# Softmax values in two f32r passes, projections in quarters, sink attention ahead of the latent heads

## The chip, the cores and the metric

One core of one Trainium2 chip runs the whole kernel in one launch. The metric is the device time of one execution in microseconds; the median of three runs counts. Engines are named as in the profile: PE is TensorE, with PEld its weight loads, DVE VectorE, ACT ScalarE, POOL GpSimd, SP the queue that issues the DMAs.

## The reference, cut to what matters

Two decoder layers over 512 tokens of width 1024, all in float32. Each layer is a mixing block and a SwiGLU feed-forward of width 2816, with RMS norms before and after each. Layer 0 mixes with eight heads of windowed softmax attention (heads A, width 64) and four heads of gated linear attention (B). Layer 1 mixes with eight query heads over two key-value heads with a window of 128 and a sink logit (C, the sink attention), and with eight latent heads (D). For heads A and D the part that the change touches is, per head:

```python
# A: a table holds slope * distance and the logarithm of how many of three patterns see a key
# D: a table holds the causal mask
s = q @ k.T * scale - table
p = softmax(s)                 # 512 queries x 512 keys, causal
o = p @ v                      # v: 512 x 64
# D: queries and keys come from latents
q = rmsnorm(h @ w_q_latent) @ w_uq      # latent of 384 = 3 tiles of 128
k, v = rmsnorm(h @ w_kv_latent) @ w_ukv # latent of 256 = 2 tiles of 128
# and k gets a rotary part that all heads share
```

## The kernel before

Activations are held transposed: 1024 channels as 8 tiles of 128 partitions, 512 tokens in the free dimension. Nearly every product is made to float32 accuracy from two float32r parts: `split` casts a tensor to f32r on ACT (the high part) and subtracts that from the source on DVE (the low part), and `mm3` adds three products, high-high, high-low, low-high. `proj` makes 128 outputs for all tokens with 24 matmuls of 512 columns. Weights come by DMA on SP into `raw` (4 buffers), are split two items ahead of use (`weights`, `fill`), and lie in `wt` (8 buffers) in the order of the list `items`.

Heads A and D go through `Units`: each head has four units, one per block of 128 queries, over the 1 to 4 key blocks up to it. The first step (`head_first`) makes the scores (PE, for A in two f32r passes over stacked parts, for D in f32), adds the table and takes the row minimum (DVE), exponentiates with a row sum (ACT), takes the reciprocal and scales the row (DVE, line 401). The second step (`head_second`) transposes each block on PE (line 407, f32) and copies it out of PSUM (ACT, line 409). The third step multiplies with the values (line 413): f32, the stationary operand is V of one head, 64 columns, the moving one 128 queries, one matmul for each key block. An f32 matmul runs as two instructions. The two heads of a pair fill the two halves of one bank, which is then split for the output projection. The second step runs `LAG` = 4 units behind the first, the third `LAG2` = 2 behind the second.

In layer 0 the query and key projections of the next pair come in one block of 48 matmuls after the third unit of a pair (`A_NEXT`). In layer 1 the latents, the shared rotary key, the sink queries, keys and values, and the latent values come first, then heads D with one unit of the sink attention (8 units, four heads and a query block each) after every third unit, and the projections of the next pair after its fourth unit (`C_EVERY`, `D_NEXT`).

The order written is a priority. The framework schedules each engine's instructions with it: a later instruction whose inputs are ready and that has a buffer may go ahead of an earlier one that waits. The order is fixed when the program is built; at run time each engine works through its list in order and waits by semaphores. Buffers that matter: PSUM has 8 banks, two under the tag `ps` (projections, the first token block of an output projection) and six under `pa` (scores, transposes, values); SBUF has 28 cells of 128 x 512 (`CELLS`) for queries, keys, probabilities, latents and most of what is short-lived; 8 pages of 4 x 512; two gain buffers of 1024.

After the heads, `out_rows` multiplies the mixed heads with the output weights: three rows of weights over all token blocks, and the last five token block by token block, so that norms of one block run beside products of the next.

## Time and profile before

| | us |
|---|---|
| median of three runs | 1229.32 (1229.27 to 1230.81) |
| profiled execution, first to last instruction | 1227.8 |
| PE busy | 1213.7 |
| DVE busy | 551.7 |
| ACT busy | 472.2 |
| POOL busy | 56.5 |

The profiled execution's own time is its span, 1227.8 us; what lies around a span is in the runs' times and not in it. Busy time is the union of an engine's instructions; since matmuls overlap, PE's says only that it is never without one. The softmax of layer 0 lies at about 155 to 235 us, that of layer 1 at about 716 to 819 us; the feed-forwards fill most of the rest.

### The profile page before, as it was taken

The page shows a single profiled execution, that of the slowest core. Times are in us where ns is not written, and L with a number is a line of the kernel's source. Part 1 is how long each engine was busy: PE and PEld are TensorE (multiplying, and loading weights), DVE is VectorE, ACT ScalarE, POOL GpSimd, SP SyncE. Part 2 cuts the span into 40 slices and gives each one's busy share as a digit, 9 for nine tenths or more (in the row PEclk, how much of TensorE's full clock was granted, in tenths as well). Part 3 has the DMA queues.
Part 4 walks back from the last instruction along what each step waited for, and adds up shares of the span by engine and source line. Part 5 has one row for each costly group of instructions (what it writes and reads, how often), then busy time and mean ns, then how long its engine had stood idle before and what let it go on. Part 6 is the DMA issues. An engine that isn't in the chain of part 4 may idle for free.

```text
span 1227.8 us, 15007 instructions
## 1 busy us (share of the span) xinstructions
PE 1213.7 (99%) x5952; PEld 1000.5 (81%) x5952; DVE 551.7 (45%) x963; ACT 472.2 (38%) x858; POOL 56.5 (5%) x91
## 2 busy tenths in 40 slices
PE   8999999999999999999999999999999999999997
PEld 6787777789888888888889877778988888888886
DVE  5633566554333333323355577866433333332313
ACT  5424465633332322312235457764323233232211
POOL 2000111010000000000010011101000000000000
PEclk9999999999999999999999999999999999999999
DMA  7432121223233233233503230032232323323311
GB/s 272 124 100 72 35 70 52 82 74 103 88 102 99 90 103 94 95 103 106 186 1 104 97 107 22 19 108 81 87 89 100 104 89 100 103 86 103 114 41 69
DMA packets 32760, 112.76 MB, mean 92 GB/s; under 512 B 4753, under 2 KB 4913, under 8 KB 32690
## 3 DMA queue, kind: packets, MB, share of 16 engines
q1 hardware_dynamic: 32690, 111.80, 28.8%
q8 instruction: 47, 0.77, 0.3%
q14 instruction: 23, 0.19, 0.0%
HBM read 109.69 MB, written 2.10 MB: 91 GB/s over the span
## 4 chain that ended last, share of the span: by engine, by line
PE 96%; DVE 2%; ACT 1%; issue 0%; DMA 0%; POOL 0%; DVEq 0%; POOLq 0%; SPq 0%; ACTq 0%
PE pg L195 12%; PE pg L193 12%; PE pg L194 12%; PE y L194 9%; PE y L195 9%; PE y L193 9%; PE avt L413 4%; PE sc L378 3%; PE pf L194 2%; PE pf L195 2%; PE pf L193 2%; PE pt L407 1%; PE pq L193 1%; PE pq L194 1%; PE tp L257 1%; PE pq L195 1%
## 5 line engine op out<-in xcount | busy, mean ns | idle before, releaser
L109 ACT CAST whi<-raw 128x1024 fp32r<-128x1024 f32 (+2 forms) x211 | 198.4, 955 | 508.5 <-PE pg L194 300.1
L110 DVE TENSOR_TENSOR wlo<-raw,whi 128x1024 fp32r<-128x1024 f32 (+2 forms) x210 | 230.3, 1111 | 336.1 <-ACT whi L109 324.9
L193 PE MATMUL pg<-hf0h,whi 128*128 128x512 f32 x320 | 124.5, 389 | 0.0
L193 PE MATMUL pg<-hf1h,whi 128*128 128x512 f32 x320 | 124.5, 389 | 0.0
L194 PE MATMUL pg<-hf1l,whi 128*128 128x512 f32 x320 | 124.5, 389 | 0.0
L194 PE MATMUL pg<-hf0l,whi 128*128 128x512 f32 x320 | 124.5, 389 | 0.0
L195 PE MATMUL pg<-hf0h,wlo 128*128 128x512 f32 x320 | 124.5, 389 | 0.0
L195 PE MATMUL pg<-hf1h,wlo 128*128 128x512 f32 x320 | 124.5, 389 | 0.0
L328 DVE TENSOR_TENSOR sg<-sg,pg 128x512 f32<-128x512 f32 x40 | 27.5, 688 | 135.4 <-PE pg L195 135.4
L193 PE MATMUL y<-whi,gh 128*128 128x512 f32 x224 | 87.1, 389 | 0.0
L194 PE MATMUL y<-wlo,gh 128*128 128x512 f32 x224 | 87.1, 389 | 0.0
L195 PE MATMUL y<-whi,gl 128*128 128x512 f32 x224 | 87.1, 389 | 0.0
L195 PEld LDWEIGHTS pg<-hf0h,wlo 128*128 128x128 f32 x320 | 60.1, 188 | 12.6
L194 PEld LDWEIGHTS pg<-hf1l,whi 128*128 128x128 f32 x320 | 60.1, 188 | 12.5
L194 PEld LDWEIGHTS pg<-hf0l,whi 128*128 128x128 f32 x320 | 60.1, 188 | 12.5
L193 PEld LDWEIGHTS pg<-hf1h,whi 128*128 128x128 f32 x320 | 60.1, 188 | 12.4
L195 PEld LDWEIGHTS pg<-hf1h,wlo 128*128 128x128 f32 x320 | 60.1, 188 | 12.3
L193 PEld LDWEIGHTS pg<-hf0h,whi 128*128 128x128 f32 x320 | 60.1, 188 | 12.2
L230 POOL TENSOR_TENSOR rs<-ms,mhalf 128x1 f32<-128x1 f32 x32 | 17.7, 554 | 851.2 <-DVE ms L228 851.2
L270 ACT ACTIVATE junk<-y 128x512 f32<-128x512 f32 x32 | 19.1, 597 | 86.4 <-PE y L195 84.9
L193 PE MATMUL y<-whi,gph 128*128 128x512 f32 x128 | 50.0, 390 | 0.0
L195 PE MATMUL y<-whi,gpl 128*128 128x512 f32 x128 | 49.8, 389 | 0.0
(337 smaller groups left out, 2291.2 us busy)
## 6 DMA issues: line engine op xcount, KB each, us to landing
raw<-in_gu_dram SPq DMA_DIRECT2D x88, 512.0 KB, 3.5
raw<-in_ffn_w_down_dram SPq DMA_DIRECT2D x44, 512.0 KB, 3.5
raw<-in_w0s_dram SPq DMA_DIRECT2D x16, 512.0 KB, 3.5
raw<-in_w1s_dram SPq DMA_DIRECT2D x11, 512.0 KB, 3.5
raw<-in_w0m_dram SPq DMA_DIRECT2D x8, 512.0 KB, 3.8
raw<-in_ab_w_out_dram SPq DMA_DIRECT2D x8, 512.0 KB, 3.5
raw<-in_cd_w_out_dram SPq DMA_DIRECT2D x8, 512.0 KB, 3.5
x<-in_x_dram SPq DMA_DIRECT2D x4, 512.0 KB, 5.9
```

The source lines that it names most:

```text
L109: nc.scalar.copy(hi, src)
L110: return (eng or nc.vector).tensor_tensor(out=lo, in0=src, in1=hi.bitcast(F32), op=ALU.subtract)
L193: nc.tensor.matmul(ps, wh, xh, start=first, stop=False)
L194: nc.tensor.matmul(ps, wh, xl, start=False, stop=False)
L195: nc.tensor.matmul(ps, wl, xh, start=False, stop=last)
L230: nc.gpsimd.tensor_tensor(out=r, in0=t, in1=mhalf, op=ALU.pow)
L257: nc.tensor.transpose(ps[:, k, :], h[:, tok(4 * i + k)], ident)
L270: nc.scalar.activation(junk, ys[j], AF.Square, scale=1.0 / 32, accum_out=ss[:, i:i + 1])
L328: nc.vector.tensor_tensor(out=t, in0=t, in1=pu, op=ALU.mult)
L378: nc.tensor.matmul(sc, q, k, start=(i == 0), stop=(i == len(ks) - 1))
L407: nc.tensor.transpose(pt[:, j, :], p[:, tok(j)], ident)
L413: nc.tensor.matmul(out_ap, v(j), t[:, j, :], start=(j == 0), stop=(j == qb))
```

## The change

The values of heads A and D become f32r. V of each head is split into a tile of 128 columns, high part beside low part, so that one stationary operand holds both; the transposed probabilities are split into high and low parts as well, and each is multiplied with it (`values`, two passes). The upper 64 rows of the result then hold the high part's product and the lower 64 the low part's; a copy on ACT and an add on DVE fold them. Two query blocks go at once: 256 columns, 128 for the last key block, which only the later query block sees. The scaling of the rows goes from DVE to POOL (`normalise`, a product of two SBUF operands); one of two key copies in `stack_k` goes from POOL to ACT. Projections are cut in steps of two of the eight channel tiles (`proj_steps`), and `Units.add` runs some of these pieces after each unit. In layer 1 the sink queries come first; the sink units come next, with the latents, the rotary key, the latent values and the first pair's projections as pieces between them (five to a unit, lags `LAG_C` and `LAG2_C`); heads D follow, with the next pair's three projections as pieces after their units 0, 2 and 4. V of heads A takes the gain buffers for two token blocks and four cells for the others.

```diff
+LAG_C = 2
+LAG2_C = 1
...
-C_EVERY = 3
-A_NEXT = 2
-D_NEXT = 3
...
-    items += w1[6:11] + [(d["w1r"], (NKD, 4, 32), "stack")] + w1[0:6]
+    items += w1[0:6] + w1[9:11] + w1[6:9] + [(d["w1r"], (NKD, 4, 32), "stack")]
...
+    def proj_steps(name, hT, finish, tag="ps"):
+        st = []
+        def step(i):
+            if not st:
+                st.extend((weights(), bank(name, tag)))
+            w, ps = st
+            for k in (2 * i, 2 * i + 1):
+                mm3(ps, part(w, ALL, k, ALL), hk(hT, k, ALL), k == 0, k == NKD - 1)
+            if i == 3:
+                finish(ps)
+        return [lambda i=i: step(i) for i in range(4)]
...
-            nc.gpsimd.tensor_copy(kh[a][oth], kh[a][own].bitcast(F32))
+            nc.scalar.copy(kh[a][oth], ps[own])
...
-        nc.vector.tensor_scalar(out=p[:, :nk], in0=p[:, :nk], scalar1=st[:, 2:3], scalar2=None, op0=ALU.mult)
+        normalise(p[:, :nk], st[:, 2:3], nk)
...
     def head_units(pr, qs, ks, tabs, v, mix):
         res = []
-        avt = []
+        us = []
         for a in range(2):
+            h = 2 * pr + a
+            avt, parts = [], []
             for qb in range(NT):
                 def first(a=a, qb=qb):
-                    if not avt:
-                        avt.append(bank("avt"))
                     return head_first(qs[a], ks[a], qb, tabs[a])
-                def second(p, a=a, qb=qb):
-                    values = head_second(p, qb, lambda j: v(j, 2 * pr + a), avt[0][a * 64:a * 64 + 64, tok(qb)])
+                def second(p, a=a, h=h, qb=qb, avt=avt, parts=parts):
+                    g, odd = qb // 2, qb % 2
+                    if not odd:
+                        parts[:] = [(cell("pth", F32R, (P, 2, 2 * P)), cell("ptl", F32R, (P, 2, 2 * P))) for _ in range(g + 1)]
+                    mine = list(parts)
+                    pt = bank("pt", "pa", (P, 4, P))
+                    for j in range(qb + 1):
+                        nc.tensor.transpose(pt[:, j, :], p[:, tok(j)], ident)
+                    for jj, hl in enumerate(mine):
+                        n = min(2, qb + 1 - 2 * jj)
+                        split(*(t[:, :n, tok(odd)] for t in hl), pt[:, 2 * jj:2 * jj + n, :])
                     def third():
-                        values()
-                        if a == 1 and qb == NT - 1:
-                            split(mix[0][:, pr, :], mix[1][:, pr, :], avt[0])
+                        if not odd:
+                            return
+                        if not avt:
+                            avt.append(bank("avt"))
+                        for j in range(2 * g + 2):
+                            o = P if j == 2 * g + 1 else 0
+                            values(avt[0][:, 2 * g * P + o:2 * (g + 1) * P], v(j, h),
+                                   [t[:, j % 2, o:2 * P] for t in mine[j // 2]], j == 0, j == 2 * g + 1)
+                        if qb == NT - 1:
+                            if a == 0:
+                                us.append(cell("u"))
+                            t = cell("fold")
+                            nc.scalar.copy(t[0:64, :], avt[0][64:128, :])
+                            nc.vector.tensor_tensor(out=us[0][a * 64:a * 64 + 64, :], in0=avt[0][0:64, :], in1=t[0:64, :], op=ALU.add)
+                            if a == 1:
+                                hi, lo = mix()
+                                split(hi[:, pr, :], lo[:, pr, :], us[0])
...
+            self.pieces = []
+        def add(self, first, second, pieces, lags):
             self.q[0].append((first(), second))
-            self.drain(LAG, LAG2)
+            self.work(pieces)
+            self.drain(*lags)
+        def work(self, n):
+            while n > 0 and self.pieces:
+                self.pieces.pop(0)()
+                n -= 1
...
-    va = [cell("va") for _ in range(NT)]
+    va = []
     for tb in range(NT):
-        (nc.scalar.copy if tb % 2 else nc.vector.tensor_copy)(va[tb], pv[tb])
+        src = pv[tb].rearrange("p (h c) -> p h c", c=64)
+        if tb < 2:
+            t = sb.tile([P, 8, P], F32R, name="va", tag="gain", bufs=2)
+            split_v(t, src)
+            va.append([t[:, h, :] for h in range(8)])
+        else:
+            ts = [cell("va", F32R, (P, 4, P)) for _ in range(2)]
+            for i, t in enumerate(ts):
+                split_v(t, src[:, 4 * i:4 * i + 4, :])
+            va.append([ts[h // 4][:, h % 4, :] for h in range(8)])
...
-    def proj_qk(pr):
...
+    def proj_qk(pr, res):
+        def q_done(ps):
+            tabs = temp("tabs", (P, 2, S))
+            nc.sync.dma_start(tabs, d["tabA"][pr])
+            qs = cell("qe", F32R), cell("qo", F32R)
+            stack_q(ps, qs)
+            res.extend((qs, tabs))
+        def k_done(ps):
+            ks = [[cell("ks", F32R) for _ in range(2)] for _ in range(2)]
+            stack_k(ps, *ks)
+            qs, tabs = res
+            res[:] = [qs, [[k[a] for k in ks] for a in range(2)], [tabs[:, a, :] for a in range(2)]]
+        return proj_steps("pq", hT, q_done) + proj_steps("pk", hT, k_done)
...
-        for i, u in enumerate(head_units(pr, *cur, lambda j, h: va[j][:, h * 64:(h + 1) * 64], mixa)):
-            un.add(*u)
-            if i == A_NEXT and pr < 3:
-                nxt = proj_qk(pr + 1)
+        nxt = []
+        if pr < 3:
+            un.pieces = proj_qk(pr + 1, nxt)
+        for u in head_units(pr, *cur, lambda j, h: va[j][h], lambda: mixa):
+            un.add(*u, 2 if len(un.pieces) > 4 else 1, (LAG, LAG2))
...
-    def latent(pss, n, g0):
...
+    def latent(n_tiles, n, g0, res):
+        zs, pm = [], []
+        def done(ps):
+            if not zs:
+                pm.append(bank("pm", "pa"))
+            i = len(zs)
+            zs.append(cell("z"))
+            nc.scalar.copy(zs[i], ps)
+            add_squares(pm[0], zs[i], i == 0, i == n_tiles - 1)
+        def norm(j):
+            if j == 0:
+                pm.append(cell("rl"))
+                nc.scalar.activation(pm[1], pm[0], AF.Ln, scale=1.0 / n, bias=epscol)
+                nc.scalar.activation(pm[1], pm[1], AF.Exp, scale=-0.5)
+            z = zs[j]
+            nc.vector.scalar_tensor_tensor(out=z, in0=z, scalar=gl[:, g0 + j:g0 + j + 1], in1=pm[1], op0=ALU.mult, op1=ALU.mult)
             hl = cell("ch", F32R), cell("cl", F32R)
-            split(*hl, u)
+            split(*hl, z)
             res.append(hl)
-        return res
...
+        steps = []
+        for _ in range(n_tiles):
+            steps += proj_steps("pl", hT, done)
+        return steps, [lambda j=j: norm(j) for j in range(n_tiles)]
     qc = page("qce"), page("qco")
-    for i in range(4):
-        ps = bank("pqc", "ps")
-        proj(ps, weights(), hT)
+    for i, ps in enumerate(split_start(4, hT, later)):
         stack_q(ps, [q[:, i, :] for q in qc])
-        if i == 2:
...
+    def key_rope():
+        rk = cell("rk")
+        nc.sync.dma_start(rk, d["ropek"])
+        em = cell("em", shape=(P, P))
+        nc.sync.dma_start(em, d["fold"])
+        ps = bank("pkr", "ps")
+        proj_stack(ps, weights(), hT)
+        nc.vector.tensor_tensor(out=rk, in0=rk, in1=ps, op=ALU.mult)
+        rks.extend((rk, em))
+    def key_fold():
+        rk, em = rks
+        ps = bank("pkp", "ps")
+        nc.tensor.matmul(ps, em, rk, start=True, stop=True)
+        khp = page("khp", F32)
+        for i in range(2):
+            nc.scalar.copy(khp[64:128, 2 * i, :], ps[64:128, :])
+            nc.vector.tensor_copy(khp[0:64, 2 * i + 1, :], ps[0:64, :])
+        khs.append(khp)
...
+    def values_d(tb):
+        if tb == 0:
+            vds.extend([weights()] + [page("vd").rearrange("p t (h c) -> p t h c", c=P) for _ in range(2)])
+        w = vds[0]
         ps = bank("pvd", "ps")
         for k in range(2):
             mm3(ps, part(ck[k], ALL, tok(tb)), part(w, ALL, k, ALL), k == 0, k == 1)
-        (nc.scalar.copy if tb % 2 else nc.vector.tensor_copy)(vd[:, tb, :], ps)
...
+    qtab, tabD = [], []
+    def proj_d(pr, res):
         o = 2 * (pr % 2)
-        qh = []
-        for a in range(2):
+        st = []
+        def query(a):
+            if not st:
+                res.extend(([], [[khs[0][:, o + i, :]] for i in range(2)]))
+                if not qtab:
+                    for i in range(2):
+                        qtab.append(cell("qtab"))
+                        nc.sync.dma_start(qtab[i], d["qtab"][:, i, :])
+                    tabD.append(cell("tabD"))
+                    nc.sync.dma_start(tabD[0], d["tabD"])
+                res.append([tabD[0], tabD[0]])
+                st.append(weights())
             ps = bank("pq", "ps")
             for k in range(3):
-                mm3(ps, part(wq, ALL, k, a, ALL), cq[k], k == 0, k == 2)
...
+                mm3(ps, part(st[0], ALL, k, a, ALL), cq[k], k == 0, k == 2)
+            qh = cell("qh")
+            nc.vector.tensor_tensor(out=qh, in0=qtab[a], in1=ps, op=ALU.mult)
+            res[0].append(qh)
+        def key():
+            if not wks:
+                wks.append(weights())
+            ps = bank("pk", "ps")
+            for k in range(2):
+                mm3(ps, part(wks[0], ALL, k, pr, ALL), ck[k], k == 0, k == 1)
+            khp = khs[0]
+            nc.scalar.copy(khp[0:64, o, :], ps[0:64, :])
+            nc.vector.tensor_copy(khp[64:128, o + 1, :], ps[64:128, :])
+        return [key, lambda: query(0), lambda: query(1)]
     un = Units()
-    un.add(*swa.pop(0))
-    cur = proj_d(0)
+    cur = []
+    kv, kv_norm = latent(2, 256, 3, ck)
+    q, q_norm = latent(3, 384, 0, cq)
+    vs = [lambda tb=tb: values_d(tb) for tb in range(NT)]
+    un.pieces = kv + q[0:2] + kv_norm + q[2:] + [key_rope, q_norm[0], vs[0], q_norm[1], vs[1], q_norm[2], vs[2], key_fold, vs[3]] + proj_d(0, cur)
+    each = -(-len(un.pieces) // len(swa))
+    for u in swa:
+        un.add(*u, each, (LAG_C, LAG2_C))
+    un.work(len(un.pieces))
+    mixd = []
+    def mix_d():
+        if not mixd:
+            mixd.extend((page("mixdh"), page("mixdl")))
+        return mixd
     for pr in range(4):
-        for i, u in enumerate(head_units(pr, *cur, lambda j, h: vd[:, j, h * 64:(h + 1) * 64], mixd)):
...
+        nxt = []
+        if pr < 3:
+            un.pieces = proj_d(pr + 1, nxt)
+        for i, u in enumerate(head_units(pr, *cur, lambda j, h: vds[1 + h // 4][:, j, h % 4, :], mix_d)):
+            un.add(*u, 1 if i in (0, 2, 4) else 0, (LAG, LAG2))
         cur = nxt
-    while swa:
-        un.add(*swa.pop(0))
```

## Rows read from the trace of the kernel before

**Rows 1.** Page, busy time of each engine, share of the span, instructions.

```profile
PE 1213.7 (99%) x5952; PEld 1000.5 (81%) x5952; DVE 551.7 (45%) x963; ACT 472.2 (38%) x858; POOL 56.5 (5%) x91
```

**Rows 2.** Windows of three stretches; columns: stretch, busy by engine, clock, DMA.

```profile
155.00:235.00 80.00, 79.71 (x450) 61.66 (x449) 49.15 (x154) 47.69 (x122) 8.66 (x12) 1.00 0.16 47
640.00:716.00 76.00, 76.00 (x434) 66.48 (x434) 39.50 (x53) 36.10 (x56) 6.15 (x10) 1.00 0.32 98
716.00:819.00 103.00, 102.02 (x575) 76.29 (x574) 78.47 (x276) 71.65 (x213) 14.79 (x16) 1.00 0.13 42
```

**Rows 3.** Timeline of TensorE, layer 0's softmax: start, us, instructions merged.

```profile
207.00 0.65 PE L413 MATMUL avt<-pts,va 128*64 128x128 f32 x4
207.58 0.44 PE L378 MATMUL sc<-ks,qo 128*128 128x128 f32 x2
207.86 0.29 PE L407 MATMUL pt<-ident,p 128*128 128x128 f32 x1
208.08 0.87 PE L413 MATMUL avt<-pts,va 128*64 128x128 f32 x6
208.88 0.51 PE L378 MATMUL sc<-ks,qo 128*128 128x256 f32 x2
...
213.02 0.43 PE L413 MATMUL avt<-pts,va 128*64 128x128 f32 x2
213.39 0.73 PE L378 MATMUL sc<-ks,qo 128*128 128x512 f32 x2
213.96 0.62 PE L195 MATMUL y<-whi,mixbl 128*128 128x512 f32 x2
```

**Rows 4.** Timeline of TensorE, f32r products of 512, 256 and 128 columns.

```profile
183.31 0.62 PE L378 MATMUL sc<-ks,qe 128*128 128x512 f32 x2
183.77 0.60 PE L407 MATMUL pt<-ident,p 128*128 128x128 f32 x4
...
640.74 0.28 PE L193 MATMUL pf<-hbh,whi 128*128 128x256 f32 x1
...
641.09 0.28 PE L193 MATMUL pf<-hbh,whi 128*128 128x256 f32 x1
...
716.98 0.39 PE L378 MATMUL sc<-kc,qce 128*128 128x128 f32 x2
717.20 0.39 PE L378 MATMUL sc<-kc,qco 128*128 128x128 f32 x2
...
767.31 0.27 PE L407 MATMUL pt<-ident,p 128*128 128x128 f32 x1
767.34 0.48 PE L390 MATMUL avt<-pth,vc 128*128 128x512 f32 x1
767.65 0.40 PE L390 MATMUL avt<-ptl,vc 128*128 128x512 f32 x1
```

**Rows 5.** Groups of VectorE and ScalarE (L401, L409: layer 0's softmax): busy, mean ns.

```profile
L110 DVE TENSOR_TENSOR wlo<-raw,whi 128x1024 fp32r<-128x1024 f32 x162 | 199.3, 1230 | 324.1 <-ACT whi L109 312.9 <-PE pkp L710 2.1 <-PE pt L407 2.1
...
L110 DVE TENSOR_TENSOR mixcl<-u,mixch 128x256 fp32r<-128x256 f32 x8 | 3.4, 423 | 7.0 <-ACT mixch L109 7.0
...
L401 DVE TENSOR_SCALAR p<-p,st 128x128 f32<-128x128 f32 (+3 forms) x32 | 12.3, 386 | 0.7
...
L409 ACT COPY pts<-pt 128x128 f32<-128x128 f32 (+3 forms) x32 | 13.1, 421 | 9.0 <-PE pt L407 8.8
...
L781 ACT COPY fold<-avt 64x512 f32<-64x512 f32 x8 | 4.7, 583 | 1.7 <-PE avt L390 1.5
```

**Rows 6.** Timeline of VectorE and GpSimd at one meeting in layer 1.

```profile
731.04 0.69 DVE L819 TENSOR_TENSOR qh<-qtab,pq 128x512 f32<-128x512 f32 x1
731.64 0.48 DVE L401 TENSOR_SCALAR p<-p,st 128x512 f32<-128x512 f32 x1
732.04 2.06 DVE L110 TENSOR_TENSOR wlo<-raw,whi 128x1024 fp32r<-128x1024 f32 x1
...
730.79 2.23 POOL L762 TENSOR_TENSOR p<-p,rden 128x512 f32<-128x512 f32 x2 [8.59 <-ACT p L383]
```

## What I predict, before the changed kernel ran

> **What bounds the kernel now.** Read the busy line of the page first [rows 1]: TensorE is busy for 1213.7 of 1227.8 us, VectorE for 551.7, ScalarE for 472.2. Then the windows of the two softmax stages [rows 2]. From 155 to 235 us (layer 0) TensorE is busy in 79.71 of 80 us, VectorE in 49.15, ScalarE in 47.69; from 716 to 819 us (layer 1) in 102.02 of 103 us, against 78.47 and 71.65. It is idle for 0.3 us and 1.0 us there. So TensorE sets the time in both stages, and nothing else does; time can come only from TensorE work that goes away, and it is lost again where another engine becomes the slower one. The reader should therefore look not at busy sums of TensorE (its matmuls overlap) but at the step from one start to the next in the timeline.
>
> **The values, as they are.** For one head there are 20 f32 instructions with 64 weight columns, in four groups of 2, 4, 6 and 8. In the timeline the group of 2 takes 213.02 to 213.39, of 4 207.00 to 207.58, of 6 208.08 to 208.88 [rows 3]: 0.37, 0.58 and 0.80 us, a step of 0.22 for each two, so 1.02 for the 8. Sum 2.77 us a head. The group costs more at its edges. On entry: the single transpose at 207.86 holds TensorE for 0.22 us before a group, where one ahead of a 128-column product takes 767.31 to 767.34 and leaves that product 0.31 instead of 0.24 to do, together 0.11 [rows 3, 4]: about 0.10 a group. On leaving: two score matmuls of 128 and of 512 columns take 0.28 and 0.57 us behind a group [rows 3], and 0.22 and 0.46 elsewhere [rows 4]: 0.06 and 0.11, and 0.10 each for the two sizes between, so 0.37 a head. One head: 2.77 + 0.40 + 0.37 = 3.54 us.
>
> What differs at the edges is the 64 in "128*64" rather than the type: the transpose at 767.31, f32 as well with 128 weight columns, is left without them [rows 4]. The Trainium skill (TensorEngine Tiling (Array Packing), Tiling Modes) says that a change of the tiling mode drains TensorE; the 0.10 us on either side agree with it, and without those edges a head would be 2.77 us and the gain 16 x 0.77 = 12 us less.
>
> **The values, as they will be.** Eight instructions of 256 columns and four of 128 a head, f32r, 128 weight columns. Three of 256 columns take 640.74 to 641.09, 0.12 each; two of 128 take 716.98 to 717.20, 0.11 each [rows 4]. 8 x 0.12 + 4 x 0.11 = 1.40 us, no edges. That the pace of 0.12 fails to hold is bounded by the f32 price, 0.22 for 128 columns: that would be 4.4 us, but no f32r row goes at it. Gain 2.14 us a head; 16 heads: **34.2 us**. Nothing else on TensorE changes in count: transposes, scores, projections, latents, sink attention are the same instructions in another order. So TensorE alone would give 1229.3 - 34.2 = 1195.1. (The profiled span is 1227.8; the runs' median 1229.32 holds 1.5 us around it, which I leave as it is.)
>
> **What the other engines get.** *VectorE, a head:* normalise goes to GpSimd, 12.3 / 8 = -1.54 us [rows 5]; the low parts of the transposed probabilities come, four pieces of 256 columns at 0.42 and two of 128 between half of that and all of it, at most 2.5, I take 2.25; the fold's add comes, 512 columns, 0.69 [rows 5, 6]. Together +1.4. VectorE's instructions overlap by about 0.09 (one begins at 731.04, takes 0.69, the next begins at 731.64 [rows 6]), and there are some three more a head, so +1.15 of its time, +9 us a stage. Layer 0: 49.2 + 9 = 58 us. TensorE's share there falls from 80 to 80 - 17.1 = 63. VectorE goes from 61% to 92%. *ScalarE, a head:* the copy of transposed values, 13.1 / 8 = 1.64 [rows 5], becomes casts in six pieces (no dearer than VectorE's, about 2.1), the fold's copy is 0.58 [rows 5]; three projections' key halves come over from GpSimd, two of the fold's size each: 47.7 + 8 x 1.0 + 3.5 = 59, less overlaps about 57 of 63 us. Layer 1 (640 to 819): VectorE 118 + 9 + 3 (value splits, rope copies moved from GpSimd) = 130 of TensorE's 161; ScalarE 108 + 12 = 120. On average there is room, but the latent heads now stand alone, and their units load VectorE as those of layer 0 do.
>
> *GpSimd* gets 32 normalises a stage. Two of 512 columns span 2.23 us [rows 6]; a head would be some 2.8 us, 22 of 63 us: not the bound. But it lengthens each chain by about 0.6 us, and in the one place where such a product meets a split of two SBUF operands, that split takes 2.06 us [rows 6], 0.83 more than the mean of 1.23 over 162 of its kind [rows 5]. Six splits in layer 0, some ten in layer 1: 0 to 13 us of VectorE time, I take a third, 2 us and 3 us. The Trainium skill (SBUF - State Buffer, SBUF: two separate sides) speaks of an exclusive lock between GpSimd and a VectorE operation with two SBUF inputs; this row agrees, and it is the rule against this change.
>
> **Order and buffers.** Projections in quarters and sink units ahead of latent heads change no count; what they do is fill. Sink units get five pieces each, mostly quarters of 6 products of 0.23 us [rows 4], about 7 us of TensorE beside each unit: so slow a beat that their chains are hidden. Latent heads lose the sink units between them and have three pieces a pair. The value parts of two token blocks take the gain buffers, so the two gain loads of the next block wait for the last values; they are used after 3 x 24 products of 0.23 us, 16 us later, and cost nothing (without this cover, one landing). Tables for the latent queries are now loaded at their first use, behind SP's weight loads; TensorE has value pieces and key products meanwhile: 0 to 2 us. Cells: 28; in the latent stage about 18 are held (latents 10, tables 3, queries 4, fold), a head's parts take up to 6, the probabilities in flight 5. That is about all of them, so a unit sometimes waits for a cell.
>
> **The sum.** Idle of TensorE, unseen in the trace of before, between 0 and what VectorE could add. Before, at 61% and 76% of VectorE, it was 0.3 and 1.0 us [rows 2]. At 92% I take 4 us for layer 0 (0.13 a unit), 4 for the latent heads, 2 for the sink stage. 1195.1 + 10 = **1205 us**.
>
> **Rivals.**
> *All of it arrives* (0.22): queues run ahead far enough, and rows of the output projection, already pulled between units at 213.96 [rows 3], fill what is left. 1193 to 1199, say 1196. Against it: two engines above 90% with short lags.
> *VectorE and ScalarE set the pace* (0.22): every split meets a normalise, 13 us, and the stages run at some 66 to 70 us instead of 63 and likewise in layer 1. Half of the gain is left: 1211 to 1223, say 1217. For it: the row of 2.06 us. By the rule of the skill on the lock, this is the case that would come out.
> *Slower* (0.06): the cells. A unit holds its cell from softmax to transposes, the parts until the values; five instructions of 0.4 to 1.1 us [rows 5, 6] with the waits between them, some 5 us. If buffers let fewer than two units overlap, TensorE waits in each of 64 units. It decides from 34.2 / 64 = 0.53 us of idle a unit on; at 0.7 it is 1195 + 45 = 1240. Against it: 18 + 10 of 28 still leaves four units in flight.
> *No difference* (0.02): the same at 0.53.
> The forecast itself (0.48) has 1200 to 1210. Faster by over 0.2% (2.5 us, about what a measurement of this kernel tells from nothing) 0.92, within 0.02, slower 0.06. The range 1194 to 1221 leaves out the slow case and the ends of the two next to it.
>
> **What would show it.** Value instructions read 128*128, steps of 0.12 and 0.11 us, no longer first score behind them; TensorE's time between first score and last value of layer 0 near 67 us, VectorE over 85% there; TensorE waits in the softmax stages of about 10 us in all, on VectorE's low parts or GpSimd's products; splits of 2 us where they meet GpSimd. Wrong it would be if the waits exceed 20 us, if the clock, granted at 1.00 in all these windows [rows 2] (2.4 GHz), falls to 1.2 GHz in idle stretches, or if 256-column products behind transposes don't keep 0.12.

## The result, and the profile after

The changed kernel takes 1216.32 us, median of 4 runs (1216.3 to 1217.78), against 1230.07 us for the kernel before, timed beside it: a ratio of 0.990 (95% interval 0.9885 to 0.9913). It is faster, by 13.8 us where 24 were forecast; it lies inside the range, and close to the time of the rival in which VectorE and ScalarE set the pace. The profiled execution has a span of 1214.7 us.

The page's busy line of the kernel after, which answers to [rows 1]:

```profile
PE 1189.9 (98%) x5824; PEld 986.9 (81%) x5824; DVE 577.7 (48%) x1023; ACT 494.6 (41%) x932; POOL 95.2 (8%) x141
```

TensorE lost 128 instructions and 24 us of busy time, but the span shrank by 13: nearly half of what was freed came back as idle time. To see where, cut the execution at four starts that both kernels have. The timeline of TensorE before (start, us, instruction), at the first score of layer 0 and the first products of the feed-forward, of layer 1 and of its feed-forward:

```profile
155.97 0.51 PE L378 MATMUL sc<-ks,qe 128*128 128x128 f32 x3
276.89 0.28 PE L193 MATMUL pf<-hf0h,whi 128*128 128x256 f32 x1
859.34 0.28 PE L193 MATMUL pf<-hf1h,whi 128*128 128x256 f32 x1
```

The third of the four, 640.74, stands in [rows 4]. And after:

```profile
154.84 0.33 PE L392 MATMUL sc<-ks,qe 128*128 128x128 f32 x2
266.47 0.28 PE L192 MATMUL pf<-hf0h,whi 128*128 128x256 f32 x1
630.32 0.28 PE L192 MATMUL pf<-hbh,whi 128*128 128x256 f32 x1
846.13 0.28 PE L192 MATMUL pf<-hf1h,whi 128*128 128x256 f32 x1
```

**Stage 0** (softmax and output of layer 0) went from 120.9 to 111.6 us, -9.3. The feed-forward between is 363.85 us in both. **Stage 1** (all mixing of layer 1) went from 218.6 to 215.8, only -2.8. The rest, about 1 us, lies ahead of stage 0.

Windows of the kernel after answer to [rows 2] (stretch, its length, then busy time of PE, PEld, DVE, ACT, POOL, clock, DMA): the softmax heads of layer 0, the sink stage of layer 1 from its first score to the first value of a latent head, and the latent heads alone.

```profile
154.80:226.40 71.60, 68.11 (x385) 55.37 (x384) 56.98 (x176) 53.75 (x148) 26.39 (x38) 1.00 0.17 53
...
668.30:755.50 87.20, 80.30 (x397) 63.02 (x395) 67.80 (x187) 62.04 (x163) 20.89 (x21) 1.00 0.26 80
755.50:805.70 50.20, 48.74 (x279) 37.84 (x278) 43.17 (x147) 37.51 (x114) 20.34 (x27) 1.00 0.07 22
```

TensorE stood idle for 0.3 and 1.0 us in [rows 2]; now it is idle for 3.5, 6.9 and 1.5 us. Most of it is in the sink stage, the one the forecast had called covered. The values themselves look as forecast. The timeline of TensorE in layer 0, against [rows 3]:

```profile
182.80 0.38 PE L437 MATMUL pt<-ident,p 128*128 128x128 f32 x2
182.93 0.36 PE L404 MATMUL avt<-pth,va 128*128 128x256 f32 x1
183.14 0.28 PE L404 MATMUL avt<-ptl,va 128*128 128x256 f32 x1
183.25 0.29 PE L404 MATMUL avt<-pth,va 128*128 128x256 f32 x1
183.38 0.28 PE L404 MATMUL avt<-ptl,va 128*128 128x256 f32 x1
183.50 0.28 PE L404 MATMUL avt<-pth,va 128*128 128x256 f32 x1
183.62 0.28 PE L404 MATMUL avt<-ptl,va 128*128 128x256 f32 x1
183.73 0.23 PE L404 MATMUL avt<-pth,va 128*128 128x128 f32 x1
183.80 0.27 PE L404 MATMUL avt<-ptl,va 128*128 128x128 f32 x1
183.91 0.39 PE L392 MATMUL sc<-ks,qo 128*128 128x384 f32 x1
```

256 columns step by 0.12 us; two of 128 take 0.18 together. The first product behind the transposes steps by 0.21, but the two transposes ahead of it by 0.13 together, so nothing is lost there.

Now the sink stage: what TensorE waits for, in its own timeline (first fence), what VectorE does at that time (second fence), and GpSimd (third).

```profile
719.32 0.28 PE L392 MATMUL sc<-kc,qco 128*128 128x256 f32 x1
719.44 0.60 PE L807 MATMUL pt<-ident,p 128*128 128x128 f32 x4
721.16 1.10 PE L850 MATMUL pkp<-rk,em 128*128 128x512 f32 x2 [1.12 <-issue]
723.49 0.50 PE L404 MATMUL avt<-pth,vc 128*128 128x512 f32 x1 [1.23 <-DVE ptl L109]
```

```profile
719.25 0.74 DVE L741 SCALAR_TENSOR_TENSOR z<-z,gl,rl 128x512 f32<-128x512 f32 x1
719.91 0.15 DVE L794 TENSOR_TENSOR den<-den,rden 128x4 f32<-128x4 f32 x1
719.98 0.68 DVE L109 TENSOR_TENSOR cl<-z,ch 128x512 fp32r<-128x512 f32 x1
720.59 0.17 DVE L795 RECIPROCAL rden<-den 128x4 f32<-128x4 f32 x1
720.67 0.39 DVE L109 TENSOR_TENSOR vd<-pvd,vd 128x256 fp32r<-128x256 f32 x1
720.98 1.52 DVE L109 TENSOR_TENSOR cl<-z,ch 128x512 fp32r<-128x512 f32 x1
722.43 0.41 DVE L109 TENSOR_TENSOR vd<-pvd,vd 128x256 fp32r<-128x256 f32 x1
722.76 1.27 DVE L109 TENSOR_TENSOR ptl<-pt,pth 128x512 fp32r<-128x512 f32 x2
```

```profile
720.92 2.48 POOL L798 TENSOR_TENSOR p<-p,rden 128x512 f32<-128x512 f32 x2 [12.23 <-DVE rden L795]
```

The transposes of a sink unit end by 720.04 and ScalarE's casts of them by 721.66, but the split `ptl` that its values need begins only at 722.76: VectorE, never idle, first does the norms and splits of the latents and of their values. One of these splits is drawn out from 0.68 to 1.52 us, just where GpSimd runs two products of two SBUF operands. TensorE loses 2.35 us in two waits. The second, of 1.23 us, is for `ptl`; for the first, of 1.12 us, the profile names no releaser, but it ends 0.10 us behind VectorE's split of `vd` at 720.67, which reads a bank of the tag that `pkp` takes as well.

The same holds for the whole stage. TensorE's idle time in it is 6.9 us, and during 6.3 of these VectorE is busy, against 67.8 of 87.2 us on average. That average doesn't decide by itself: the latent heads have VectorE busy in 43.17 of 50.20 us, a larger share, and only 1.5 us of idle time. VectorE's work in the sink stage comes in bunches; the worst ten microseconds are these, with 7.03 us of TensorE and 9.67 of VectorE:

```profile
720.00:730.00 10.00, 7.03 (x36) 5.23 (x36) 9.67 (x26) 7.65 (x20) 2.48 (x2) 1.00 0.20 55
```

So much the trace shows; whether VectorE's load, the order, or the values' own side work is the cause is what the experiments tell apart.

### The profile page after: what moved, and what is told of

It is laid out like the page before. It is cut to its first block, busy times and chain, and to the rows that moved or that the text cites. A ratio compares the mean times of both kernels' runs of the same rounds, so it can differ in the third digit from the quotient of the medians.

```text
span 1214.7 us, 15055 instructions
## 1 busy us (share of the span) xinstructions
PE 1189.9 (98%) x5824; PEld 986.9 (81%) x5824; DVE 577.7 (48%) x1023; ACT 494.6 (41%) x932; POOL 95.2 (8%) x141
## 4 chain that ended last, share of the span: by engine, by line
PE 88%; DVE 6%; ACT 4%; issue 1%; POOL 0%; DMA 0%; DVEq 0%; POOLq 0%; SPq 0%; ACTq 0%
PE pg L194 12%; PE pg L193 12%; PE pg L192 12%; PE y L193 9%; PE y L194 9%; PE y L192 9%; PE pf L193 2%; PE pf L194 2%; PE pf L192 2%; PE sc L392 1%; ACT p L397 1%; PE avt L404 1%; PE tp L271 1%; PE pq L192 1%; DVE p L395 1%
## 5 line engine op out<-in xcount | busy, mean ns | idle before, releaser
L193 PE MATMUL y<-wlo,gh 128*128 128x512 f32 x224 | 87.2, 389 | 0.0
L192 PE MATMUL y<-whi,gh 128*128 128x512 f32 x224 | 87.2, 389 | 0.0
L194 PE MATMUL y<-whi,gl 128*128 128x512 f32 x224 | 87.2, 389 | 0.0
L193 PEld LDWEIGHTS pg<-hf1l,whi 128*128 128x128 f32 x320 | 60.1, 188 | 12.5
L193 PEld LDWEIGHTS pg<-hf0l,whi 128*128 128x128 f32 x320 | 60.1, 188 | 12.5
L192 PEld LDWEIGHTS pg<-hf0h,whi 128*128 128x128 f32 x320 | 60.1, 188 | 12.5
L194 PEld LDWEIGHTS pg<-hf1h,wlo 128*128 128x128 f32 x320 | 60.1, 188 | 12.3
L194 PEld LDWEIGHTS pg<-hf0h,wlo 128*128 128x128 f32 x320 | 60.1, 188 | 12.3
L400 POOL TENSOR_TENSOR p<-p,st 128x128 f32<-128x128 f32 (+1 forms) x64 | 47.3, 747 | 80.0 <-DVE st L414 76.0
```

The costliest lines, as they stand in the source:

```text
L192: nc.tensor.matmul(ps, wh, xh, start=first, stop=False)
L193: nc.tensor.matmul(ps, wh, xl, start=False, stop=False)
L194: nc.tensor.matmul(ps, wl, xh, start=False, stop=last)
L400: nc.gpsimd.tensor_tensor(out=p, in0=p, in1=r.to_broadcast([P, n]), op=ALU.mult)
```

## The experiments

Two notes on reading them. Stages are cut as above, each length in one profiled execution. In some executions the profile grants TensorE a clock of 0.50 (1.2 GHz) for stretches of 3.4 us (three times 6.8), with no change to the kernel there: before has one such stretch (from 145 us), after none, and the experiments none to four, apart from the last microseconds of every execution, which are in no stage. The stage lengths below have half of each stretch taken out. Where TensorE is busy throughout that is about right (the last section shows one, which cost 1.5 us); where it waits for others as well, it is the most that a stretch can cost. So in stage 1 the lengths of old_order_new_values may be up to 5.1 us too short, of old_order_lag_3_2 up to 3.4, and of normalise_on_vector, squares_and_low_parts, no_side_work and sinks_earlier up to 1.7; no conclusion below turns on that. The feed-forward between the two stages, which no edit touches, agrees within 0.1 us in all of these kernels, and stage 0 is 111.5 to 111.7 us in all that have layer 0 as in after. The medians are as measured.

| kernel | median us | ratio to before (95%) | stage 0 | stage 1 |
|---|---|---|---|---|
| before | 1230.07 | 1 | 120.9 | 218.6 |
| after | 1216.32 | 0.9899 (0.9885-0.9913) | 111.6 | 215.8 |
| layer0_only | 1220.41 | 0.9940 (0.9925-0.9955) | 111.5 | 218.7 |
| order_f32_values | 1228.11 | 0.9997 (0.9987-1.0008) | 111.7 | 225.7 |
| old_order_new_values | 1228.78 | 0.9999 (0.9987-1.0010) | 111.5 | 220.6 |
| old_order_lag_3_2 | 1229.06 (one run) | | 111.5 | 221.9 |
| normalise_on_vector | 1222.27 | 0.9959 (0.9946-0.9972) | 113.3 | 219.4 |
| low_parts_on_gpsimd | 1224.39 | 0.9954 (0.9937-0.9970) | 112.8 | 219.1 |
| squares_and_low_parts | 1222.38 | 0.9944 (0.9927-0.9960) | 112.7 | 216.9 |
| squares_one_piece_later | 1217.85 | 0.9906 (0.9889-0.9924) | 111.5 | 215.7 |
| third_step_later | 1219.27 | 0.9915 (0.9900-0.9930) | 113.3 | 215.7 |
| pieces_spread | 1221.09 | 0.9939 (0.9921-0.9957) | 111.7 | 217.4 |
| no_normalise | 1214.70 | 0.9883 (0.9861-0.9904) | 110.7 | 215.1 |
| no_fold | 1215.43 | 0.9889 (0.9866-0.9912) | 109.6 | 216.1 |
| no_low_part_split | 1216.00 | 0.9894 (0.9869-0.9918) | 109.0 | 215.1 |
| no_side_work | 1215.61 (one run) | | 108.4 | 213.7 |
| sink_no_low_part | 1212.66 (one run) | | 111.6 | 210.5 |
| sinks_earlier | 1222.70 | 0.9952 (0.9935-0.9968) | 111.7 | 219.4 |
| sink_f32_values | 1212.33 | 0.9867 (0.9848-0.9885) | 111.5 | 209.5 |
| sink_f32_and_squares | 1212.68 | 0.9877 (0.9858-0.9896) | 111.5 | 210.7 |

### The change in its parts

**layer0_only**: the section of layer 1, its list of weights and its `head_units` are those of before.

```
-    items += w1[0:6] + w1[9:11] + w1[6:9] + [(d["w1r"], (NKD, 4, 32), "stack")]
+    items += w1[6:11] + [(d["w1r"], (NKD, 4, 32), "stack")] + w1[0:6]
```

> Layer 0 as changed; layer 1 in the order of the kernel before, with its f32 values of 64 weight columns and its normalise on VectorE. In the traces the first block ends 10.4 us earlier after the change than before. Both theories: about 1219.7 us (1230.1 - 10.4), that is within 2 us; the rest of the change, in layer 1, is then worth only about 3 us in all.

**order_f32_values**: as after, but the latent heads take before's `head_units`:

```
-            vds.extend([weights()] + [page("vd").rearrange(...) for _ in range(2)])
+            vds.extend([weights(), page("vd", F32)])
...
-        for i in range(2):
-            split_v(vds[1 + i][:, tb], src[:, i])
+        (nc.scalar.copy if tb % 2 else nc.vector.tensor_copy)(vds[1][:, tb, :], ps)
```

> Layer 0 as changed, layer 1 in the new order (sink units with the latent pieces, then latent heads alone), but with the f32 values, the copy of transposed probabilities and the normalise on VectorE of the kernel before. Theory ORDER (the new order of layer 1 itself makes TensorE wait some 10 us, by piling the latents' VectorE work and the sink units' chains on one stretch): some 10 us above layer0_only, about 1229. Rival SIDE WORK (the order costs nothing; the stalls come from the splits, folds and GpSimd products that the new values bring): within 2 us of layer0_only, about 1220.

1220.41 and 1228.11 us: ORDER. With the same f32 values stage 1 goes from 218.7 to 225.7: the new order, with the pieces and the copies that go with it, costs 7.0 us by itself, and the new values then take 9.9 off (225.7 to 215.8). The windows of order_f32_values show where (sink stage, latent heads):

```profile
668.40:752.50 84.10, 78.85 (x394) 62.97 (x392) 67.22 (x183) 60.06 (x155) 16.30 (x16) 1.00 0.25 83
752.50:811.50 59.00, 58.97 (x328) 40.53 (x327) 35.82 (x124) 33.74 (x94) 0.00 (x0) 1.00 0.05 19
```

Nearly all of TensorE's idle time in stage 1, 5.25 of 5.4 us, is in the sink stage; the latent heads with f32 values have none. layer0_only has 1.0 us of idle time in all of stage 1, so 4.4 of the 7.0 us show as idle time and the rest as longer steps, which the trace doesn't place. Cut behind the last value product of the sink units, where both kernels have issued the same 649 instructions of TensorE, the new values save 12.3 us behind the cut and cost 2.5 ahead of it, where V's splits now stand.

**old_order_new_values**, **old_order_lag_3_2**: before's order of layer 1 with the new values. That would need nine pages, and there are eight, so the sink units come early and `mixd` gets its pages behind them:

```
-C_EVERY = 3
+C_EVERY = 1
...
-        un.add(*u)
+        un.add(*u, 0, (4, 1) if swa else (LAG, LAG2))
```

(in the second kernel (3, 2) in place of (4, 1)).

> Layer 0 as changed; layer 1 in the order of the kernel before (latents first, projections whole, sink units between latent heads) with the new f32r values; sink units come one behind each of the first seven latent units instead of every third, and third steps one unit behind the second instead of two, because pages and cells do not hold more. Theory ORDER: the 17.1 us of layer 1's values arrive but for some 4: 1204 to 1209. Rival SIDE WORK: the stalls stay, 1213 to 1218.

> As old_order_new_values, but while sink units are left the second step stands three units and the third two units behind (instead of four and one), so that the values are not right behind the transposes. Layer 1's stage was 220.6 us there with the slow clock stretches taken out, 218.7 with f32 values in the order of before. If the short third step made that: 208 to 213. If the order of before leaves VectorE too much to do beside the cheaper values: 216 to 220.

Stage 1: 220.6 and 221.9 us. The first missed both theories; its trace had TensorE waiting for the transposes' copies, right behind which the short lag had put the values, so the second was made. With the longer lag it is no better, and its 221.9 us lie beyond both of its alternatives, nearest to the one by which VectorE gets too much to do. Neither of these two placements carries the new values. Windows of old_order_lag_3_2 from its first latent score on:

```profile
717.00:760.00 43.00, 35.58 (x193) 27.54 (x192) 33.95 (x123) 31.04 (x98) 14.96 (x18) 0.96 0.11 38
760.00:811.00 51.00, 45.95 (x233) 33.72 (x234) 42.23 (x142) 36.53 (x109) 19.27 (x26) 0.97 0.10 32
```

TensorE idles for 12.5 of 94 us, 3.1 of them in waits for GpSimd's products of the sink units and most of the rest in waits for VectorE; which of the two engines decides was not taken apart. Before's exact spacing, every third unit, was not tried with the new values.

### What the side work of the new values costs

```
no_normalise:       -        normalise(p[:, :nk], st[:, 2:3], nk)
no_fold:            -  nc.scalar.copy(t[0:64, :], avt[0][64:128, :])
                    -  nc.vector.tensor_tensor(out=us[0][...], in0=avt[0][0:64, :], in1=t[0:64, :], op=ALU.add)
                    +  split(hi[own, pr, :], lo[own, pr, :], avt[0][0:64, :])
no_low_part_split:  -  split(*(t[:, :n, tok(odd)] for t in hl), pt[...])
                    +  nc.scalar.copy(hl[0][:, :n, tok(odd)], pt[...])
```

no_side_work makes all three edits.

> The kernel after without the product that normalises the probabilities of the softmax units (left out in both layers; the sink units keep theirs). It prices GpSimd's part of the chain. Stages after: layer 0 softmax and output 111.6 us, layer 1 mixing 215.8 us. If GpSimd's latency or its meetings with VectorE make the stalls: 3 us or more shorter each. If not: under 1 us each.

> The kernel after without the fold: the two value halves are not added, the split is made from the first half alone (the low part of V is left out of the result). It takes 0.58 us of ScalarE and 0.69 us of VectorE a head away and lets the bank of the values go one step earlier; TensorE's instructions are the same. If the bank held for the fold makes the stalls (1.7 to 2.1 us of waits for the fold a stage in the trace of after): 2 us shorter in each stage. If those waits only stand for a late VectorE: under 1 us.

> The kernel after without the low parts of the transposed probabilities in the softmax heads: both value products read the high part, so TensorE's instructions are the same, and VectorE loses 2.2 us a head, about 18 us a stage. If the split on VectorE makes the stalls of both stages: layer 0 104 to 107 us instead of 111.6, layer 1 209 to 212 instead of 215.8. If the sink stage has its stalls by itself: layer 0 as said, layer 1 only 2 to 4 us shorter.

> The kernel after without normalise, without fold and without the low parts of the transposed probabilities in the softmax heads (left out of the result; the second value product reads the high part again). TensorE's instructions are those of after. One by one these shortened layer 0's stage (111.6 us) by 0.9, 2.0 and 2.6 us and layer 1's (215.8 us) by 0.7, -0.3 and 0.7. If they are separate prices: 106 and 214.7 us. If they cover for one another (any one left keeps the stalls): layer 0 at 103 to 105, near the 103.8 that TensorE's count gives, and layer 1 at 210 to 212.

Taken out alone, they shorten stage 0 by 0.9, 2.0 and 2.6 us and stage 1 by 0.7, -0.3 and 0.7; together by 3.2 and 2.1. GpSimd's part is small. In layer 0 the fold and the split matter, but the prices overlap: together they are less than the sum (5.5), so neither form of the last expectation came out. no_low_part_split missed both forms of its expectation too. In stage 1 the side work of the heads isn't what is missing.

### More or less on VectorE, by way of GpSimd

**normalise_on_vector** (the first two lines) and **low_parts_on_gpsimd** (the others, in the softmax stages):

```
-        normalise(p[:, :nk], st[:, 2:3], nk)
+        nc.vector.tensor_scalar(out=p[:, :nk], in0=p[:, :nk], scalar1=st[:, 2:3], scalar2=None, op0=ALU.mult)
...
-        ins = split(hi, lo, raw, None if made else nc.gpsimd)
+        ins = split(hi, lo, raw, nc.gpsimd if side[0] or not made else None)
...
-            split(*hl, z)
+            split(*hl, z, nc.gpsimd)
```

and the same for the split of `us[0]`. squares_and_low_parts adds the edit of squares_one_piece_later (below).

> The kernel after, with the normalise of the softmax units of 128 to 512 columns back on VectorE in both layers. Rival GPSIMD (the longer chain through GpSimd and its meetings with VectorE's splits make the stalls): 4 to 8 us faster than the kernel after, 1208 to 1212. Theory ORDER and rival SIDE WORK: VectorE gets 12.3 us a stage back, where it is already near full; 3 to 10 us slower, 1219 to 1226.

> The kernel after, with those low parts that need nothing from PSUM made on GpSimd during the softmax stages: the weights' (128 x 1024, 1.23 us on VectorE, 2.38 us on GpSimd), the mixed heads' and the latents'. VectorE gets some 10 us a stage less, GpSimd some 20 us more. Theory PACE (VectorE's load sets the softmax stages): 4 to 8 us faster than after, 1208 to 1212. Rival CHAIN (each unit's chain through VectorE, ScalarE and GpSimd is too long for its lag; load is not the matter): no gain, or 1 to 5 us slower, since products of 2.4 us now stand ahead of normalises on GpSimd, 1216 to 1221.

> Both edits of squares_one_piece_later and low_parts_on_gpsimd together. LOCAL WAITS and PACE both right: 1206 to 1210. If they are one and the same loss seen at two places: no better than the better of the two.

All lose in stage 1: 219.4, 219.1 and 216.9. The first gives VectorE 12.3 us of instructions a stage, and they cost 1.7 and 3.6 us, the 3.6 behind the sink stage: up to the last value of a sink unit, the slow stretch taken out, the two kernels agree within 0.1 us. So the heads' normalise on GpSimd isn't what makes the waits, and the rival GPSIMD falls. The second goes against PACE as I had put it, but its groups of VectorE show that load isn't simply moved to GpSimd (mean ns; first after, then low_parts_on_gpsimd):

```profile
L741 DVE SCALAR_TENSOR_TENSOR z<-z,gl,rl 128x512 f32<-128x512 f32 x5 | 4.5, 917 | 1.5 <-ACT rl L739 1.5
...
L109 DVE TENSOR_TENSOR sql<-sq,sqh 128x512 fp32r<-128x512 f32 x5 | 4.1, 823 | 4.3 <-ACT sqh L108 4.3
```

```profile
L744 DVE SCALAR_TENSOR_TENSOR z<-z,gl,rl 128x512 f32<-128x512 f32 x5 | 6.9, 1387 | 4.0 <-ACT rl L742 4.0
...
L109 DVE TENSOR_TENSOR sql<-sq,sqh 128x512 fp32r<-128x512 f32 x5 | 5.3, 1065 | 11.1 <-ACT sqh L108 11.1
```

The operations on the latents' chain, whose two inputs are both in SBUF, took half as long again and 29% longer. What GpSimd took over it partly charged to VectorE, and 2.8 of the 3.3 us lost lie ahead of the last value of a sink unit. The Trainium skill (SBUF - State Buffer, SBUF: two separate sides) has an exclusive lock between the two for such operations; these rows agree with it.

### The place of single instructions

**squares_one_piece_later**: the two sums-of-squares products of a latent tile come ahead of the second quarter of the next tile's projection:

```
-            steps += proj_steps("pl", hT, done)
+            st = proj_steps("pl", hT, done)
+            steps += st[0:1] + [lambda f=st[1]: (sums(), f())] + st[2:]
```

> The kernel after, with the two sums-of-squares products of each latent tile put one projection quarter later, so that they no longer stand right behind the projection whose squares ScalarE and VectorE must first make. In the trace of after TensorE waits 1.7 us for the high parts of the squares and 0.9 us for the low parts. Theory LOCAL WAITS (the sink stage's stalls are single instructions put too early): 2 to 3 us faster than after, about 1214. Rival PACE (VectorE is the slower engine in that stage; a wait taken out at one place comes back at the next): within 0.8 us of after.

Stage 1: 215.7, no gain. The scheduler of the build sets the final order, and the products moved by a few instructions only, so this says little against LOCAL WAITS. TensorE's waits for the high and low parts went from 1.8 to 1.5 us, and one of 1.1 us for a sink unit's reciprocal was new.

**third_step_later** and **pieces_spread** (the list of weights follows its order):

```
-LAG2 = 2
+LAG2 = 3
...
-    un.pieces = kv + q[0:2] + kv_norm + q[2:] + [key_rope, q_norm[0], vs[0], ..., key_fold, vs[3]] + proj_d(0, cur)
+    un.pieces = kv + q[0:4] + kv_norm + [key_rope] + q[4:6] + [vs[0]] + q[6:8] + [vs[1], key_fold] + q[8:10] + [vs[2]] + q[10:12] + [vs[3]] + q_norm + proj_d(0, cur)
```

> The kernel after, with the third step of a head's unit (values and fold) three units behind its second step instead of two, in both layers. Theory CHAIN: the waits of the values for the parts of the transposed probabilities go, 1 to 3 us faster than after, 1213 to 1215. Theory PACE: no lag makes a full engine faster, within 1 us of after.

> The kernel after, with the sink stage's pieces in another order: the light ones (norm of the key latents, rope product, value pieces, fold of the rope) stand between the projection quarters of the query latents instead of behind all of them, so that the last sink units have projection quarters beside them too. Stage from the first product of layer 1 to its feed-forward: 215.8 us after. Theory TAIL (the last sink units have too little TensorE work beside them, since the heavy quarters come first): 3 to 6 us shorter, 210 to 213. Rival: the stalls follow the sink units' own chains and move with them: within 1 us of 215.8.

215.7 and 217.4 in stage 1, and 113.3 in stage 0 with the longer lag. Neither a later third step of the heads nor projection quarters beside the last sink units helps: TAIL falls, and CHAIN for the heads. `LAG2` is the heads' lag; that of the sink units, `LAG2_C`, was not changed, so a later third step in the sink stage itself is untried, and so is another order of VectorE's own instructions there. Waits moved from one place to the next, as they would behind an engine that is short of time.

### VectorE's load in the sink stage itself

**sink_no_low_part**, in `swa_second`:

```
-            hl = cell("pth", F32R, (P, 4, P)), cell("ptl", F32R, (P, 4, P))
-            split(*hl, pt)
+            hl = (cell("pth", F32R, (P, 4, P)),) * 2
+            nc.scalar.copy(hl[0], pt)
```

> The kernel after without the low parts of the transposed probabilities in the sink units (both value products read the high part; TensorE's instructions are the same): 14 splits of 512 columns, 9.6 us of VectorE, leave the sink stage. Layer 1's stage is 215.8 us after. Theory VECTOR LOAD (the sink stage stalls because VectorE has more to do there than TensorE): 4 to 6 us shorter. Rival ORDER OF CHAINS (waits are for chains in which VectorE is only the last link): under 2 us.

**sinks_earlier**: the first four projections are two of the sink queries, `kc` and `vc`; the other two sink queries become pieces:

```
-    un.pieces = kv + q[0:2] + kv_norm + ...
+    un.pieces = qcs[0] + kv + qcs[1] + q[0:2] + kv_norm + ...
```

> The kernel after with the sink units begun earlier: the first four projections of layer 1 are the queries of the first four sink units, the sink keys and values; the other two query projections become pieces among the sink units. From 630 to 668 us VectorE is busy in 20 of 38 us after the change, in the sink stage in 26 of 30. If the sink stage stalls for want of TensorE work beside VectorE's: 3 to 5 us shorter than 215.8. If the stalls come from the latents' chain at the end of that stage, which this leaves in place: within 1 us.

210.5: 5.3 us less, for 9.6 us of VectorE's work in that stage. That is VECTOR LOAD, and the one edit so far that moved stage 1 by what was missing. The edit also takes a link out of each unit's chain, since the values no longer wait for a split, and frees a cell for each key block. The waits tell the link from the load: of TensorE's idle time in the sink stage of after, two waits of 1.2 and 0.4 us were for a removed split, and they are gone; but so are 1.1 us ahead of `pkp`, 1.0 for the fold's add and 1.0 in four smaller waits, for instructions that the edit leaves in place (against that, 0.6 us of other waits came). ScalarE's work stayed the same (62.04 and 61.17 us). sinks_earlier missed both its cases: 219.4, 3.6 us longer. It spreads the sink units over more projections, but TensorE then waits 1.9 us at one place for VectorE's `khp`; why that order is worse I did not settle.

If VectorE is the limit there, taking work off it must shorten the stage even where TensorE gets some back. **sink_f32_values** takes the sink units' values back to f32 with 64 weight columns, without split and fold:

```
-            split(*hl, pt)
+            nc.scalar.copy(t, pt)
...
+            for a in range(2):
+                for i, j in enumerate(js):
+                    nc.tensor.matmul(avt[a * 64:a * 64 + 64], vc[:, j, kv * 64:(kv + 1) * 64], parts[i][:, :, a, :],
+                                     start=(i == 0), stop=(i == len(js) - 1))
+            split(mixc[0][...], mixc[1][...], avt)
```

> The kernel after, with the values of the sink units in f32 with 64 weight columns: no split of the transposed probabilities (14 x 0.68 us of VectorE), no adds of the fold (16 x 0.41 us) and none of its copies on ScalarE, so VectorE loses some 16 us in the sink stage; TensorE gets more: 14 blocks at 0.86 instead of 0.46 us and some 0.2 us a unit for the change of columns, about 7 us. Theory VECTOR LOAD: the stage's stalls of 11 us mostly go, so that layer 1's stage is 2 to 4 us shorter than 215.8 in spite of that, 212 to 214, and the kernel at 1212.5 to 1214.5. If TensorE's count rules there: 3 to 7 us longer, 219 to 223.

**sink_f32_and_squares** adds, for the latents, one f32 product instead of a split and two f32r products:

```
-            add_squares(pm[0], zs[i], i == 0, i == n_tiles - 1)
+            nc.tensor.matmul(pm[0], ones, sq, start=(i == 0), stop=(i == n_tiles - 1))
```

> As sink_f32_values, and the latents' sums of squares are made by one f32 product each instead of two f32r products, so that the two splits behind each square (0.6 us of ScalarE, 0.69 us of VectorE, five times) and two links of the chain go; TensorE gets 5 x 0.4 us more. In after TensorE waits 2.6 us for these splits. If these waits are real: 0.5 to 2 us shorter than sink_f32_values. If VectorE has room by then and the waits are covered: 1 to 2 us longer.

sink_f32_values: stage 1 in 209.5 us, 6.3 less than after and less than the 212 to 214 expected; 1212.33 us, ratio 0.9867 (0.9848 to 0.9885). TensorE has more to do, but less than expected: its steps on the sink units' values are 8.3 us instead of 7.2, not 7 us more. So this isn't the hard test that it was meant to be; it says that f32 values without side work cost TensorE little here and VectorE much less. The profiled execution had three slow stretches of the clock (5.1 us) and the span still was 1212.9; the run with a mean granted clock of 0.999, that of after, has 1208.5 against 1214.7. No kernel here that does the whole computation is faster, and only sink_f32_and_squares comes within the interval. The sink stage in windows, sink_no_low_part and then sink_f32_values, cut as that of after above:

```profile
669.90:751.90 82.00, 79.21 (x396) 62.65 (x394) 58.46 (x172) 61.17 (x162) 20.03 (x21) 1.00 0.25 78
```

```profile
672.90:753.70 80.80, 79.45 (x418) 60.52 (x416) 54.53 (x162) 57.56 (x158) 21.80 (x22) 1.00 0.27 86
```

From after (87.2 us, VectorE busy 67.80) VectorE's work falls by 9.3 and 13.3 us and the stage by 5.2 and 6.4; TensorE's idle time falls from 6.9 to 2.8 and 1.35 us. With the squares in f32 as well stage 1 is 1.2 us longer again (210.7), the second of its two cases: VectorE has room by then, and the extra product only costs TensorE.

## Why the prediction was wrong

**What failed is the term for the sink stage.** The prediction said: "Sink units get five pieces each, mostly quarters of 6 products of 0.23 us [rows 4], about 7 us of TensorE beside each unit: so slow a beat that their chains are hidden", and gave 2 us. It measured 7.0 for the order (layer0_only to order_f32_values) and 2.5 more with the new values, 9.5 in all, of which 6.9 show as idle time of TensorE. The beat was costed for TensorE alone. A sink unit has more VectorE work than TensorE work (the groups of after add up to some 39 us of VectorE for the eight units; TensorE's steps on them are 22 us before), the pieces bring the latents' norms and splits to the same engine, and VectorE serves them in order. The balance that was drawn up for VectorE, 130 us over the attention of layer 1, holds (131.4 us in the windows from 630.3 to 805.7) and hides that one part of it is bunched. That the new order would "change no count" was right and was no reason for so small a cost.

**The values, 34.2 us, were over-sized at the edges.** With the side work out (no_side_work), TensorE's steps in stage 0, summed from start to start, are 12.5 us less than before: values and transposes 33.0 to 20.1, where 14.2 was forecast, so 12.9 of it came; scores 12.3 and 12.2, where 0.37 a head, 3.0 us, was to go; projections and output 0.5 more. So the term for the scores behind a value group, read off two places of [rows 3], did not come, and stage 0 had about 12.5 to give instead of 17.1. This is a lower bound: no_side_work still has 2.0 us of idle time there, where before has 0.3. The pace of 0.12 was right, that of 0.11 a little high (0.09).

**The idle time of layer 0** was forecast at 4 us; side work made 3.2 (111.6 against 108.4), and the profile shows 3.5: about right, as was VectorE's sum there (57.0 us, forecast 58). The stretch is longer than forecast, 72.3 us from the first score to the last value instead of 67, so that VectorE's share is 80% and not over 85%. For the latent heads, 4 us forecast, 17.1 - 12.3 = 4.8 missing, which includes edges of scores that did not go; not taken apart further.

**GpSimd**, 2 and 3 us forecast for its meetings: normalise as a whole is worth 0.9 and 0.7. VectorE's weight splits in the heads of layer 0 took 1328 ns on average against 1230 in [rows 5].

**The rival with the right time had another mechanism.** It was to come from splits meeting normalises in both stages. What lengthened the run most was VectorE's load in one stage. That pace was set by VectorE there is right; "every split meets a normalise" is not: without the normalises the stages are 0.9 and 0.7 us shorter. That the time came out near this rival's is luck.

The books: -9.3 (stage 0), +7.0 (order), -9.9 (values in stage 1) and -1.1 ahead of stage 0, where before's slow stretch of the clock lies, make -13.3; the spans differ by 13.1. Of the 34.2 us, 12.1 arrived in the two stages and 22.1 are gone: 9.5 in the sink stage (2 forecast), 7.8 in layer 0 (4 forecast; 3.2 by side work, 4.6 in the values' own term), 4.8 behind the sink stage (4 forecast). Counted as idle time alone, the forecast's 10 us seem to hold, 3.5 + 6.9 + 1.5 = 11.9, but that is luck: the sink stage has 6.9 for 2 and the latent heads 1.5 for 4, and part of what was lost is in longer steps. So the prediction's own mark, waits over 20 us, was not reached. The rival of the cells, by which it would have been slower, did not come true.

## What to carry to other kernels

Cost a change of order stage by stage and engine by engine: add up, for the new neighbours, what each engine has to do in that stage, not in the layer. Work moved off TensorE is only a gain where TensorE is the limit; in a stage where TensorE waits for VectorE, the dearer f32 product without splits can be the faster one (209.5 against 215.8 us here). And when single waits move but don't vanish as instructions are shifted, take load off the suspected engine instead of shifting them again.

## What the runs showed besides

The granted clock fell to half at times with nothing in the program to set it apart. layer0_only and after issue the same instructions on TensorE up to layer 1, with starts within 0.3 us until 145.2 us. Windows of layer0_only and then of after:

```profile
132.00:138.00 6.00, 5.26 (x33) 3.74 (x32) 4.92 (x12) 2.25 (x6) 1.27 (x2) 1.00 0.29 87
138.00:145.10 7.10, 7.10 (x36) 5.53 (x37) 4.39 (x8) 2.66 (x4) 0.34 (x1) 1.00 0.04 5
145.20:148.40 3.20, 3.20 (x9) 2.50 (x9) 1.39 (x2) 2.42 (x5) 0.77 (x2) 0.50 0.44 152
```

```profile
132.00:138.00 6.00, 5.28 (x33) 3.81 (x32) 4.96 (x11) 2.13 (x6) 1.27 (x2) 1.00 0.31 87
138.00:145.10 7.10, 7.10 (x37) 5.54 (x36) 4.27 (x8) 2.79 (x4) 0.48 (x1) 1.00 0.11 10
145.20:148.40 3.20, 3.20 (x15) 2.64 (x15) 1.39 (x2) 2.29 (x4) 0.63 (x2) 1.00 0.35 142
```

9 products against 15 in the same 3.2 us, at 1.2 and at 2.4 GHz, behind seven fully busy us and six with 0.7 us of idle time in both. What decides it stays open. From one side of this stretch to the other layer0_only falls 1.5 us further behind, as much as some of the edits here, so that stages of such kernels must be compared with it taken out.
